# Mixer output and the second feed-forward block: gated sums kept as operands, output weights loaded once, turned rows put in place

## Chip, core and metric

The kernel runs on one core of a Trainium2 chip (trn2). The time is device time in microseconds (us) of one execution of the whole program. The engines are TensorE (PE, matmuls; PEld, its weight loads), VectorE (DVE), ScalarE (ACT), GpSimd (POOL) and SyncE (SP), whose queue issues all of this kernel's DMAs.

## What is computed

One layer of a streaming encoder on 1152 tokens (1024 of a prompt, 8 times 16 of samples), width 1024, all in float32 in and out. Cut to what matters here:

```python
f = swiglu(rms_norm(h, ffn1_pre_g), ffn1_w_gu, ffn1_w_down)   # d_ff 2816
h = h + 0.5 * rms_norm(f, ffn1_post_g)
# mixer: three branches ya, yb, yc out of one input projection
yb = rms_norm(y * silu(z), norm_g)                             # y: the scan
merged = gates[0] * (ya @ wa) + gates[1] * (yb @ wb) + gates[2] * (yc @ wc)
h = h + rms_norm(merged @ wo, mix_post_g)
f = swiglu(rms_norm(h, ffn2_pre_g), ffn2_w_gu, ffn2_w_down)
h = h + 0.5 * rms_norm(f, ffn2_post_g)
```

## The kernel before

Every float32 product is made of three float32r matmuls: both operands are split into a rounded part (`hi`, an ACT copy) and the rest (`lo`, a subtraction on DVE or POOL), `split`, lines 121 to 123. `mm3` issues the three, the one with `lo` weights first.

Tokens come in 9 tiles of 128, in 3 chunks of 384 (`CH`) for projections and down products, and in 2 units of 576 (`UNIT`, each of two halves of 288) for gate/up. `prenorm` normalises a token tile, and its `turn` transposes it on PE into `xT`, split. `gate_up` (line 378) makes gate and up products of one unit in seven half-size products per step (a Strassen-like scheme): per step of 128 columns, `weights` (285) loads two blocks of 0.5 MB into staging buffers and makes seven split combinations on ACT, DVE and POOL, `cell` (324) does the seven products and stores the gated result to DRAM (`hff`). The unit's operands `A0` and `A1` are made once by `operands` (261) from raw transposed rows `xr`: seven splits and four sums of 128x1152, two of these eleven steps and one further subtraction on POOL.

`down` (410) multiplies by a 1024-wide weight: for each chunk of 384 tokens it walks over blocks of k, loads 128 rows of the left operand (`hr`, split into `hh`) and of the weight (`wdraw`, split into `wd`), and runs 18 matmuls of 128x512 for each. `post` then norms each token tile, adds the residual, and `after` may begin the next norm; its transposes run two steps later (`later`, `passed`).

After the scan, `finish` (1020) loads the scan's output `yz`, norms and turns it into `ybT`, fills PE with what is left of the gate products (`filler`, 14 of 24 gates), and runs the branch projection: for each 128 columns j and chunk c, 24 matmuls, a product with the gate, a sum, and a store to DRAM (`mrg`). Then `down` reads `mrg` back, with the output weights `wo` loaded and split anew for each chunk, `lo` on POOL. The new rows are normed, transposed to `xs`, stored to DRAM (`xr`) and loaded again unit by unit for the second `gate_up`, whose first weights are made when the second chunk is done (`between`).

A planner in the framework puts each engine's instructions in order by its own estimates, in the order of the program where they are ready together; buffers of a pool go round, and a new pool's buffer waits for whoever last used that place. Pools stand on the left or right end of the memory, as named.

## Time and profile before

| | us |
|---|---|
| median of 3 runs | 2979.92 |
| lowest and highest run | 2973.94, 2980.82 |
| the profiled execution | 2983.82 |
| its span, first to last instruction | 2982.1 |

The profile's page gives busy time by engine: PE 2825.8 us (95% of the span), its weight loads 2644.9, DVE 1384.5, ACT 1007.5, POOL 847.6. The granted clock of PE was 0.975 on average. In the order of the program: first gate/up loop to about 555 us, first down to about 830, mixer to about 1830, branch projection to 2015, output projection to about 2170, second gate/up loop to 2699, second down to the end. A busy PE is not PE at its peak: what a stretch loses is read by setting its matmuls against their pace in an undisturbed stretch.

### The profile page before, as it was taken

How to read it: one execution, taken by the hardware profiler on the slowest of the kernel's cores; microseconds unless marked ns; L12 is line 12 of the kernel's file. 1: busy time of each engine (PE TensorE's matmuls, PEld its weight loads, DVE VectorE, ACT ScalarE, POOL GpSimd, SP SyncE). 2: the span in 40 equal slices, each digit the busy share in tenths (PEclk: the TensorE clock that was granted, in tenths of full speed). 3: DMA queues.
4: the chain of work that ended last, by engine and by line, in shares of the span. 5: the costliest groups of instructions: out<-in, count | busy, mean ns of one | idle time of the engine just before them, and what ended most of it. 6: DMA issues, size and time to landing. Idle time of an engine off the chain costs nothing. (4 is left out here: it accounts for less than half of the span.)

```text
span 2982.1 us, 43879 instructions
## 1 busy us (share of the span) xinstructions
PE 2825.8 (95%) x17310; PEld 2644.9 (89%) x17310; DVE 1384.5 (46%) x2039; ACT 1007.5 (34%) x1738; POOL 847.6 (28%) x909
## 2 busy tenths in 40 slices
PE   5999999999999999999999997998779999999999
PEld 4999999888899999999988886996569999997887
DVE  6444444454532243222477775422474444445553
ACT  6222222444443113211243455313442222324442
POOL 4443343100010001111066654144443434430000
PEclk8999999999999999999999998999889999999999
DMA  3222221665743114333233356665452222226662
GB/s 117 67 82 71 70 76 55 202 200 184 218 142 104 48 33 118 104 91 94 69 96 105 91 151 184 193 210 179 156 164 71 67 85 71 67 92 203 218 220 93
DMA packets 354268, 362.44 MB, mean 122 GB/s; under 512 B 24447, under 2 KB 306291, under 8 KB 354062
## 3 DMA queue, kind: packets, MB, share of 16 engines
q1 hardware_dynamic: 354061, 359.64, 39.2%
q8 instruction: 136, 2.23, 0.3%
q14 instruction: 71, 0.57, 0.1%
HBM read 280.88 MB, written 78.69 MB: 121 GB/s over the span
## 5 line engine op out<-in xcount | busy, mean ns | idle before, releaser
L204 PE MATMUL down<-wd,hh 128*128 128x512 f32 x2808 | 657.4, 395 | 40.1 <-ACT wd L122 22.2
L204 PEld LDWEIGHTS down<-wd,hh 128*128 128x128 f32 x2808 | 532.7, 191 | 158.7 <-ACT wd L122 26.4
L320 PE MATMUL pw<-A_s,w 128*128 128x288 f32 x4224 | 612.9, 301 | 29.7 <-ACT A_s L122 15.2
L320 PEld LDWEIGHTS pw<-A_s,w 128*128 128x128 f32 x4224 | 580.1, 192 | 40.1 <-ACT A_s L122 16.8
L320 PE MATMUL pw<-A,w 128*128 128x288 f32 x3168 | 457.1, 297 | 13.0 <-DVE A L123 7.7
L320 PEld LDWEIGHTS pw<-A,w 128*128 128x128 f32 x3168 | 435.7, 190 | 15.6 <-DVE A L123 8.8
L204 PE MATMUL pgate<-xT,w_hi 128*128 128x384 f32 x1152 | 295.6, 337 | 0.0
L123 DVE TENSOR_TENSOR w<-wraw,w 128x512 fp32r<-128x512 f32 x220 | 189.5, 863 | 135.2 <-ACT w L122 135.2
L123 DVE TENSOR_TENSOR wd<-wdraw,wd 128x1024 fp32r<-128x1024 f32 x132 | 161.4, 1224 | 118.8 <-ACT wd L122 117.9
L122 ACT CAST wd<-wdraw 128x1024 fp32r<-128x1024 f32 x156 | 163.3, 1050 | 153.4 <-PE down L204 94.0
L204 PEld LDWEIGHTS pgate<-xT,w_hi 128*128 128x128 f32 x1152 | 208.2, 188 | 0.6
L204 PE MATMUL pxbc<-xT,w_hi 128*128 128x384 f32 x768 | 205.5, 345 | 0.0
L204 PE MATMUL pgate<-xT,w_lo 128*128 128x384 f32 x576 | 196.9, 342 | 3.8 <-DVE w_lo L123 3.8
L123 DVE TENSOR_TENSOR w_lo<-wraw,w_hi 128x1024 fp32r<-128x1024 f32 (+1 forms) x104 | 125.5, 1206 | 123.2 <-ACT w_hi L122 110.8
L371 POOL TENSOR_TENSOR wh<-wh,wy 128x288 f32<-128x288 f32 x88 | 89.7, 1019 | 276.1 <-ACT wh L360 247.9
L122 ACT CAST w<-wraw 128x512 fp32r<-128x512 f32 x220 | 135.9, 619 | 78.0 <-PE pw L320 45.1
L161 POOL TENSOR_SCALAR post_r<-post_ss 128x1 f32<-128x1 f32 x27 | 8.1, 300 | 535.8 <-ACT junk L172 535.8
L123 DVE TENSOR_TENSOR hh<-hr,hh 128x384 fp32r<-128x384 f32 x156 | 92.4, 597 | 131.3 <-ACT hh L122 131.3
L122 ACT CAST hh<-hr 128x384 fp32r<-128x384 f32 x156 | 79.2, 512 | 214.1 <-PE down L204 164.3
L204 PEld LDWEIGHTS pxbc<-xT,w_hi 128*128 128x128 f32 x768 | 139.6, 190 | 0.9
L204 PE MATMUL pxbc<-xT,w_lo 128*128 128x384 f32 x384 | 135.8, 354 | 0.0
L345 ACT ACTIVATE wh<-pw 128x288 f32<-128x288 f32 x88 | 36.2, 411 | 280.6 <-PE pw L320 280.6
(270 smaller groups left out, 4175.0 us busy)
## 6 DMA issues: line engine op xcount, KB each, us to landing
wdraw<-in_ffn_w_down_dram SPq DMA_DIRECT2D x132, 512.0 KB
wraw<-in_ffn_w_gu_dram SPq DMA_DIRECT2D x88, 512.0 KB
wraw<-in_w_in_dram SPq DMA_DIRECT2D x80, 512.0 KB
hff<-wh SPq DMA_DIRECT2D x88, 288.0 KB
hr<-hff SPq DMA_DIRECT2D x132, 192.0 KB
wdraw<-in_w_out_dram SPq DMA_DIRECT2D x24, 512.0 KB
h<-fg SPq DMA_DIRECT2D x18, 512.0 KB
cumb<-cumd SPq DMA_DIRECT2D x36, 256.0 KB
```

Of the source, the lines that this page charges most:

```text
L122: self.nc.scalar.copy(hi, raw)
L123: return (eng or self.nc.vector).tensor_tensor(lo, raw, hi.bitcast(F32), op=ALU.subtract)
L161: nc.gpsimd.tensor_scalar(r, ss[0], ss[1], eps, op0=ALU.add, op1=ALU.add)
L204: mm = self.nc.tensor.matmul(ps, lhsT=lhs[a], rhs=rhs[b], start=first and i == 0, stop=last and i == 2)
L320: self.nc.tensor.matmul(ps[:, :HCH], lhsT=b[:, x, k], rhs=a[:, y, k], start=first and k == 0 and i == 0, stop=k == 3 and i == 2, skip_grou ...
L345: nc.scalar.activation(h[:, 0], b[2][:, :HCH], AF.Silu)
L371: nc.gpsimd.tensor_tensor(h[:, 1], h[:, 1], y, op=ALU.mult)
```

## The change

- `finish` no longer stores the gated sums. Each is split into an SBUF tile `mT` (24 tiles of 128x2x384), and `down` takes these as its left operand. The order of the last two column blocks is by chunk. Gates left over are issued ahead of each group of transposes instead of around them.
- The output weights are loaded and split once into 8 tiles `wd` (`lo` on DVE), in the place of `ybT` on the right side, ahead of `down`.
- In the tail, the normed copy goes to the buffer of the residual (`xn`) instead of over the result. Of the transposed rows, those of tokens 0 to 575 go through DRAM as before, into buffers of their own; those of tokens 576 to 1151 are written from PSUM straight to the raw rows of unit 1.
- The first weights of the second gate/up loop are made after the operands of unit 0, in the place of `wd`, instead of during the output projection.
- The last step of the second gate/up loop runs unit 0 before unit 1. `down_pools` places `hh` ahead of `wd`.
- After the mixer there are 3 staging buffers (before: 5) and 5 `aux` buffers (before: 6).

The diff, without hunks that only hand on new arguments:

```diff
...
@@ -224,11 +225,11 @@
-    def prenorm_raw(self, t, h, gcol, put):
+    def prenorm_raw(self, t, h, xn, gcol, put):
         nc = self.nc
         r = self.rsqrt(self.sumsq(h, "pre_ss"), D * EPS, "pre_r")
-        nc.scalar.activation(h, h, AF.Copy, scale=r)
+        nc.scalar.activation(xn, h, AF.Copy, scale=r)
...
@@ -248,8 +249,8 @@
-        def put(t, half):
-            c0 = t * P
+        def put(t, half, skip=0):
+            c0 = t * P + skip
             while c0 < t * P + P:
@@ -375,13 +376,13 @@
-    def gate_up(self, B, a0, second, w_gu, h_d):
+    def gate_up(self, B, a0, second, w_gu, h_d, end):
         A = [a0, None]
         for kt in range(NFF):
             if kt > 0:
                 B = self.weights(w_gu, kt * P, DFF + kt * P)
-            for u in (1, 0) if kt == NFF - 1 else (0, 1):
+            for u in end if kt == NFF - 1 else (0, 1):
                 if A[u] is None:
@@ -390,11 +391,20 @@
-    def down_pools(self, ctx, nwd, nhh=8):
+    def down_pools(self, ctx, nwd):
         self.hrp = self.pool(ctx, "hr", 3)
+        self.hhp = self.pool(ctx, "hh", 8)
         self.wdp = self.pool(ctx, "wd", nwd)
-        self.hhp = self.pool(ctx, "hh", nhh)
-        self.late, self.step = [], 0
+    def from_dram(self, h_d):
+        def hT(k, r):
+            hr = self.hrp.tile([P, CH], F32, name="hr")
+            self.nc.sync.dma_start(hr, h_d[k * P : (k + 1) * P, r * CH : (r + 1) * CH])
+            hh = self.hhp.tile([P, 2, CH], F32R, name="hh")
+            self.split(hr, hh[:, 0], hh[:, 1])
+            return hh
+        return hT
@@ -407,9 +417,15 @@
-    def down(self, h_d, w, post, blocks=DOWN_BLOCKS, wide_eng=None, between=None):
-        nc = self.nc
+    def wide(self, w, k):
+        raw = self.stage("wdraw")
+        self.nc.sync.dma_start(raw, w[k * P : (k + 1) * P, :])
+        wd = self.wdp.tile([P, 2, D], F32R, name="wd")
+        self.split(raw, wd[:, 0], wd[:, 1])
+        return wd
+    def down(self, hT, w, post, blocks=DOWN_BLOCKS):
         end = sum(blocks) - 1
@@ -419,14 +435,8 @@
                 for k in kts:
-                    hr = self.hrp.tile([P, CH], F32, name="hr")
-                    nc.sync.dma_start(hr, h_d[k * P : (k + 1) * P, r * CH : (r + 1) * CH])
-                    hh[k] = self.hhp.tile([P, 2, CH], F32R, name="hh")
-                    self.split(hr, hh[k][:, 0], hh[k][:, 1])
-                    raw = self.stage("wdraw")
-                    nc.sync.dma_start(raw, w[k * P : (k + 1) * P, :])
-                    wd[k] = self.wdp.tile([P, 2, D], F32R, name="wd")
-                    self.split(raw, wd[k][:, 0], wd[k][:, 1], wide_eng)
+                    hh[k] = hT(k, r)
+                    wd[k] = w(k)
                 last = k0 == end + 1
@@ -444,9 +454,6 @@
                     self.passed()
-            if between is not None:
-                between(r)
     def post_norm(self, banks, g, h, fg):
@@ -1017,21 +1024,34 @@
-    def finish(self, m_d):
+    def finish(self, mp):
         n, nc, io = self.n, self.nc, self.io
         ybT = n.new_xT()
-        g_y = n.gain(io["ssm_norm_g"][0], "gpre")
-        for t in range(NT):
-            if t % 3 == 0:
-                self.filler((t // 3 + 1) * KD - self.filled)
-            y = n.aux("yz")
-            nc.sync.dma_start(y, self.yz_d[t * P : (t + 1) * P, :])
-            n.prenorm(t, y, g_y, ybT, y)()
-        ws = {}
+        g_y = n.gain(io["ssm_norm_g"][0], "gpost")
+        def norms(c):
+            out = []
+            for t in range(3 * c, 3 * c + 3):
+                y = n.aux("yz")
+                nc.sync.dma_start(y, self.yz_d[t * P : (t + 1) * P, :])
+                out.append(n.prenorm(t, y, g_y, ybT, y))
+            return out
+        for c in range(2):
+            turns = norms(c)
+            self.filler((4, 5)[c] * KD // 2 - self.filled)
+            for turn in turns:
+                turn()
+        turns = norms(2)
+        self.filler(3 * KD - self.filled)
         order = [(j, c) for j in range(KD) for c in range(NCHK)]
-        order.sort(key=lambda jc: (jc[0] > 1, jc[0] < 2 and jc[1] == 2, jc))
+        order.sort(key=lambda jc: (jc[0] > 1, jc[0] < 2 and jc[1] == 2, jc[0] > 5, jc[1] if jc[0] > 5 else 0, jc))
+        ws, mT = {}, {}
         for j, c in order:
+            if c == 2:
+                while turns:
+                    turns.pop(0)()
             if j not in ws:
@@ -1043,7 +1063,9 @@
             nc.gpsimd.tensor_tensor(s, s, a, op=ALU.add)
-            nc.sync.dma_start(m_d[js, cs], s)
+            m = mT[j, c] = mp[c].tile([P, 2, CH], F32R, name="mT")
+            n.split(s, m[:, 0], m[:, 1])
+        return mT
@@ -1068,13 +1090,12 @@
                 nc.sync.dma_start(dst(t), fg)
-                return after(t, fg)
+                return after(t, fg, h)
         return post
     h_d = dram("hff", [DFF, TOK])
     xr_d = dram("xr", [D, TOK])
-    m_d = dram("mrg", [D, TOK])
     A = [None, None]
...
@@ -1122,9 +1143,9 @@
             n.down(
-                h_d,
-                io["ffn1_w_down"][0],
-                tail(io["ffn1_post_g"][0], 0.5, lambda t: rows(io, t), at(h1), lambda t, h: n.prenorm(t, h, gn, xT, h)),
+                n.from_dram(h_d),
+                lambda k: n.wide(io["ffn1_w_down"][0], k),
+                tail(io["ffn1_post_g"][0], 0.5, lambda t: rows(io, t), at(h1), lambda t, h, xn: n.prenorm(t, h, gn, xT, xn)),
             )
@@ -1151,52 +1172,65 @@
         n.banks(c0, 6)
-        n.stages(c0, 5, 6, 512)
-        cr = ExitStack()
+        n.stages(c0, 3, 5, 512)
+        n.gbp = n.pool(c0, "gb", 1)
+        cx = ExitStack()
+        xrp = n.pool(cx, "xr", 1)
+        XR = [None, {(t, k): xrp.tile(n.blk, F32, name=f"xr{t}{k}") for t in range(2) for k in range(2)}]
+        with ExitStack() as cr:
+            with ExitStack() as cl:
+                mp = [n.pool(cl, f"mT{c}", KD) for c in range(NCHK)]
+                with ExitStack() as cw:
+                    n.conv_pools(cw, "right", 4)
+                    mT = m.finish(mp)
+                ctx_x.close()
+                n.wdp = n.pool(cr, "wd", KD, "right")
+                wo = [n.wide(io["w_out"][0], k) for k in range(KD)]
+                xr0 = n.pool(cr, "xr0", 1, "right")
+                def after(t, h, xn):
+                    n0 = min(max(UNIT - t * P, 0), P)
+                    xs = n.stage("xs").rearrange("p (k c) -> p k c", k=KD) if n0 else None
+                    def put(t, half):
+                        if n0:
+                            yield xs[:, 4 * half : 4 * half + 4, :n0], 0, n0
+                        if n0 < P:
+                            for dst, a, b in n.put_units(XR)(t, half, n0):
+                                yield dst, a, b
+                    turn = n.prenorm_raw(t, h, xn, n.cols["g2"], put)
+                    def out():
+                        turn()
+                        if n0:
+                            nc.sync.dma_start(xr_d[:, t * P : t * P + n0].rearrange("(k p) c -> p k c", p=P), xs[:, :, :n0])
+                    return out
+                n.down(lambda k, r: mT[k, r], lambda k: wo[k], tail(io["mix_post_g"][0], 1.0, at(h1), at(h2), after), (4, 4))
+                n.passed(2)
+            c1 = c0.enter_context(ExitStack())
+            n.unit_pool(c1, 0)
+            XR[0] = {(t, k): xr0.tile(n.blk, F32, name=f"xq{t}{k}") for t in range(2) for k in range(2)}
+            for (t, k), v in XR[0].items():
+                nc.sync.dma_start(v, xr_d[512 * k : 512 * k + 512, t * HCH : (t + 1) * HCH].rearrange("(k p) c -> p k c", p=P))
+            A0 = n.operands(0, XR[0])
+        n.unit_pool(c1, 1)
+        n.turn_pools(c1)
+        with ExitStack() as cr:
+            n.w_pools(cr, "right")
+            B = n.weights(w_gu, 0, DFF)
+            n.gate_up(B, A0, lambda: n.operands(1, XR[1]), w_gu, h_d, (0, 1))
+        c1.close()
+        cx.close()
         with ExitStack() as c1:
-            n.gbp = n.pool(c1, "gb", 1)
-            n.down_pools(c1, 6, 6)
-            with ExitStack() as cw:
-                n.conv_pools(cw, "right", 4)
-                m.finish(m_d)
-            ctx_x.close()
-            n.unit_pool(cr, 0, "right")
-            n.w_pools(cr, "right")
-            made = {}
-            def unit(u):
-                x = n.raw_unit(u)
-                for (t, k), v in x.items():
-                    c = (2 * u + t) * HCH
-                    nc.sync.dma_start(v, xr_d[512 * k : 512 * k + 512, c : c + HCH].rearrange("(k p) c -> p k c", p=P))
-                return n.operands(u, x)
-            def after(t, h):
-                xs = n.stage("xs").rearrange("p (k c) -> p k c", k=KD)
-                turn = n.prenorm_raw(t, h, n.cols["g2"], lambda t, half: [(xs[:, 4 * half : 4 * half + 4], 0, P)])
-                def out():
-                    turn()
-                    nc.sync.dma_start(xr_d[:, t * P : (t + 1) * P].rearrange("(k p) c -> p k c", p=P), xs)
-                return out
-            def between(r):
-                if r == 1:
-                    made["B"] = n.weights(w_gu, 0, DFF)
-            n.down(m_d, io["w_out"][0], tail(io["mix_post_g"][0], 1.0, at(h1), at(h2), after), (4, 4), nc.gpsimd, between)
-            A0 = unit(0)
-            n.passed(2)
-        with ExitStack() as c1:
-            n.unit_pool(c1, 1)
-            n.turn_pools(c1)
-            n.gate_up(made["B"], A0, lambda: unit(1), w_gu, h_d)
-        cr.close()
-        with ExitStack() as c1:
-            n.gbp = n.pool(c1, "gb", 1)
             n.down_pools(c1, 8)
-            n.down(h_d, io["ffn2_w_down"][0], tail(io["ffn2_post_g"][0], 0.5, at(h2), lambda t: out_rows(io, t)))
+            n.down(
+                n.from_dram(h_d),
+                lambda k: n.wide(io["ffn2_w_down"][0], k),
+                tail(io["ffn2_post_g"][0], 0.5, at(h2), lambda t: out_rows(io, t)),
+            )
```

## Rows read from the trace of the kernel before

**Rows 1.** Stretches: length, busy us by engine, granted PE clock, DMA share, GB/s.
```profile
600.00:700.00 100.00, 99.74 (x451) 82.20 (x450) 55.41 (x69) 45.11 (x78) 6.95 (x12) 1.00 0.61 202
...
2100.00:2200.00 100.00, 63.97 (x271) 51.27 (x270) 52.52 (x53) 43.43 (x70) 46.11 (x34) 0.79 0.64 203
...
2800.00:2900.00 100.00, 100.00 (x443) 82.81 (x442) 53.31 (x65) 39.19 (x61) 2.58 (x6) 1.00 0.70 227
```

**Rows 2.** Waits of PE, 2015 to 2225 us: us in total, times, longest.
```profile
PE down L204 <- ACT wd L122: 22.2, 2, 14.2
PE down L204 <- POOL wd L123: 10.6, 8, 2.7
PE pw L320 <- DVE A_s L123: 9.1, 3, 3.6
PE pw L320 <- ACT A_s L122: 4.6, 2, 3.8
```

**Rows 3.** Stretches as in rows 1: branch projection, and the start of the second block.
```profile
1920.00:2015.00 95.00, 95.00 (x550) 95.00 (x549) 28.20 (x36) 15.09 (x18) 40.69 (x29) 1.00 0.65 199
...
2168.00:2218.00 50.00, 29.23 (x146) 26.06 (x144) 43.39 (x32) 22.51 (x29) 25.18 (x13) 0.77 0.63 191
```

**Rows 4.** Chain of work (start, length, what); stretches for tile pw; timeline of PE.
```profile
2015.23 29.29 PE down L204 x129
...
2300.00:2600.00 300.00, 300.00 (x2240) 297.86 (x2239) 60.36 (x134) 21.81 (x54) 1.00 0.24 73
...
2697.23 1.86 PE L320 MATMUL pw<-A_s,w 128*128 128x288 f32 x12 [1.04 <-DVE wy L337]
```

**Rows 5.** Timeline, 1830 to 1850 us: start, length, engine, line, operation; idle before, releaser.
```profile
1842.95 1.94 PE L195 MATMUL tp<-ident,yz 128*128 128x128 f32 x8 [12.67 <-DVE yz L186]
...
1847.79 1.22 DVE L123 TENSOR_TENSOR w_lo<-wraw,w_hi 128x1024 fp32r<-128x1024 f32 x1
```

**Rows 6.** Stretches at the two joints from gate/up to down; timeline of ACT at the second.
```profile
555.00:566.00 11.00, 7.35 (x19) 5.05 (x20) 8.41 (x11) 5.07 (x8) 1.04 (x1) 0.73 0.72 219
2699.00:2710.00 11.00, 7.55 (x19) 4.98 (x19) 9.56 (x13) 6.91 (x10) 1.05 (x1) 0.71 0.68 211
...
2702.96 1.99 ACT L122 CAST wd<-wdraw 128x1024 fp32r<-128x1024 f32 x2 [3.62 <-DMA hff<-wh]
```

**Rows 7.** Groups by line and shape, 1790 to 2260 us: busy us, mean ns; idle before.
```profile
L123 POOL TENSOR_TENSOR wd<-wdraw,wd 128x1024 fp32r<-128x1024 f32 x24 | 58.1, 2437 | 38.4 <-ACT wd L122 38.4
...
L123 DVE TENSOR_TENSOR hh<-hr,hh 128x384 fp32r<-128x384 f32 x24 | 18.6, 780 | 54.4 <-ACT hh L122 54.4
...
L122 ACT CAST hh<-hr 128x384 fp32r<-128x384 f32 x24 | 12.2, 510 | 89.6 <-PE down L204 55.6 <-DMA hr<-mrg 33.9
```

**Rows 8.** Timeline, tail of token tile 0 in the output projection.
```profile
2036.39 0.60 ACT L172 ACTIVATE junk<-down 128x512 bf16<-128x512 f32 x1 [4.24 <-PE down L204]
...
2044.51 1.09 PE L239 MATMUL tp<-ident,fg 128*128 128x128 f32 x8
...
2045.71 1.28 DVE L241 TENSOR_TENSOR xs<-tp,colsg 128x512 f32<-128x512 f32 x2
```

**Rows 9.** Timeline of PE and DVE at the start of the first block.
```profile
27.12 3.25 PE L320 MATMUL pw<-A,w 128*128 128x288 f32 x12 [4.70 <-DVE A L123]
...
57.21 0.68 DVE L241 TENSOR_TENSOR xr<-tp,colsg 128x512 f32<-128x512 f32 x1
...
80.47 6.55 PE L320 MATMUL pw<-A_s,w 128*128 128x288 f32 x48
```

**Rows 10.** Timeline of DVE and POOL at the start of the second block.
```profile
2183.54 3.61 POOL L271 TENSOR_TENSOR xr<-xr,xr 128x1152 f32<-128x1152 f32 x1 [9.90 <-DVE xr L271]
2184.63 3.73 DVE L123 TENSOR_TENSOR A_s<-xr,A_s 128x1152 fp32r<-128x1152 f32 x1
```

**Rows 11.** Timeline, weights of one late gate/up step of the second block.
```profile
2652.77 1.29 POOL L303 TENSOR_TENSOR wt<-wraw 128x512 f32<-128x512 f32 x1
...
2667.43 0.62 ACT L122 CAST w<-wt 128x512 fp32r<-128x512 f32 x1 [0.67 <-PE pw L320]
```

9 lines of the change are left out of this document (5 added, 4 removed).

## The prediction

> **What bounds the kernel now.** I read the table by stretches first. TensorE (PE) is busy all the time at full clock in the long product loops, and around 2100 us it is not: 64 of 100 us busy at clock 0.79, against 100 of 100 at 1.00 in the last block [rows 1]. This is the output projection after the mixer and the start of the second feed-forward block. The waits of PE in 2015 to 2225 us say on what: the four longest entries hold 46.5 us, 32.8 of them on the two halves of the split of `wd` (output weights), and 13.7 on operands `A_s` of the next block [rows 2]. In 2168 to 2218 VectorE (DVE) is busy 43.4 of 50 us and PE's clock stands at 0.77: operands are what ends last there [rows 3].
>
> How much is lost I take from work, not from busy time, since slow clock hides in busy time. From the first `down` matmul (2015.23) to the end of the last product of the gate/up loop (2697.23 + 1.86 = 2699.09) are 683.9 us [rows 4]. In it lie 432 `down` matmuls (8 k x 9 token tiles x 2 x 3), which in the last stage go at 100 us / 443 = 0.2257 us each [rows 1]: 97.5 us; 72 transposes of 1.09 / 8 = 0.136 us [rows 8]: 9.8 us; and 3696 `pw` matmuls (22 steps x 2 units x 7 products x 12) at 300 / 2240 = 0.1339 us [rows 4]: 495.0 us. Together 602.3, so **81.6 us are lost**, in waits and in matmuls run between them at the lower of the two clock levels (1.2 GHz, a granted clock of 0.5).
>
> Three smaller holes: 12.67 us before the first transpose after the scan, and the gate matmuls only from 1849 on, when `w_lo` is ready (1847.79 + 1.22) [rows 5]; and the two joints from gate/up to down, where 19 matmuls take 11 us: 11 - 19 x 0.2257 = 6.7 us lost at each; behind the second, the second `wd` split waits for the last store of the gated sums [rows 6].
>
> **The change part by part.**
> *Weights once, sums kept.* 16 of 24 loads of `wd`, 16 ACT casts of 1.0 us [rows 6] and 16 POOL subtractions (2.44 us) go, 8 subtractions go to DVE, 1.22 us for the same 128x1024 shape [rows 5]; 24 stores and 24 loads of the merged sums go; their 24 splits move from `down` to the branch projection [rows 7]. There they cost ACT 24 x 0.51 = 12 us and DVE 24 x 0.78 = 19 us over 95 us in which DVE was busy 28 [rows 3]: hidden; if that cover were gone, only the last tile's split (1.3 us) could reach PE, and it is first used a third of the way from the end. The 16 wd rounds are what PE waited for: the 32.8 us go with them.
> *What is late next there:* `wd` now lies where the transposed `ybT` lay. By the pool sizes and the way slots are handed out, `wd` 1 to 4 lie over the first two thirds of `ybT`, which the new order (units 6 and 7 chunk by chunk) frees four and two products before the end of the branch loop; but `wd` 0 touches the last third, free only when the last branch matmul is done. So `down` starts a cast and a subtraction late: 1.0 + 1.22 and some 0.2 of signals, 2.5 us. Bounds 0 (another slot) and 15 (its raw load late as well: the longest single wait on `wd` now was 14.2 [rows 2]). The other seven are needed at 1.4 us steps at the earliest, and their splits take 1.22.
> *`down` itself* then has per 128 tokens 48 x 0.2257 + 8 x 0.136 = 11.9 us of PE against about 4 us each of ACT and DVE. I allow 2 us of waits (0 to 8).
> *Units.* Unit 0 (tokens 0 to 575) still goes through DRAM, but its buffers no longer queue behind the tails of the last tokens; its source is complete after token tile 4, with some 25 us of `down` left, so four of seven operands can be made under it; the last two wait for the memory of kept sums that the last matmuls read, and are needed 5th and 7th. The weights of the first gate/up step move from the middle of `down` (where their loads, casts and subtractions take turns with those of `wd` on SP, ACT and POOL) to its last 16 us, over `wd` 1 to 4. Unit 1 now goes from PSUM straight to its place: two stores and two loads of DRAM per half and the queueing on SP disappear. What then ends last is the tail of token tile 8: last matmul, squares, norm, norm, transpose, copy. For tile 0 it took 2036.39 to 2046.99 = 10.6 us [rows 8]. Then unit 1's operands have to be made while PE runs unit 0's first cell (84 x 0.134 = 11.3 us). The trace has the same situation: at the start of the first block the last transposed piece of unit 1 was in place at 57.9 us (57.21 + 0.68), and 167 matmuls of the first two cells lie between the first `pw` row and 80.47, from where PE runs on; 80.47 - 168 x 0.1339 = 58.0. So the loop ran as if it had begun, unhindered, at the moment unit 1 was complete [rows 9]. I take this for the changed kernel: loop begins 10.5 us after the last `down` matmul, of which 24 transposes (3.3 us) are work already counted: 7.2 us lost, bounds 2 and 25.
> Loss of this stage: 2.5 + 2 + 7.2 = 11.7 in place of 81.6: **gain 69.9 us**.
> *A rule set against it.* A subtraction of 128x1152 on DVE, 1.37 us by its size against the 1.22 of 128x1024 [rows 5], took 3.73 while POOL ran one of 3.61 [rows 10]. The Trainium skill, page "SBUF — State Buffer", section "SBUF: two separate sides", says that DVE instructions with two SBUF inputs and GpSimd instructions take a shared port pair as an exclusive lock. The trace agrees: 3.73 is near the sum of waiting and own time. What it does to the transition is the first rival.
> *Gates ahead of turns.* Six, four, four gates go ahead of the three groups of transposes. `w_lo` no longer stands behind DVE's copies of turned rows: about 1.2 us earlier, and the gain of the post norm is loaded later, 0.5 MB less ahead of the `yz` loads; 16 transposes that stood in the hole come later. I take **1 us**, between -4 (three staging buffers instead of five, where the gates load 0.5 MB each) and 6.
> *Joints.* Behind the second block `hr`, `hh` and the first `wd` now lie over unit 1's raw rows and unit 0's operands, free early or 11 us before the end, since unit 0 now goes first at the end; nothing waits for the last store: 6.7 becomes 1.7, **gain 5** (-1 to 6.7). In the first block only the order of `hh` and `wd` changes; the second and third `wd` then wait for gate/up weights of the last products instead of the store: **gain 1.5** (-4 to 6).
> *Nothing:* the norm written beside its input, which takes a wait on a store out of a chain off the path; aux 5 for 6; the final `down` with three staging buffers in place of five: the first `down` has three, and PE is 99.7 us of 100 busy there [rows 1].
>
> Sum: 69.9 + 1 + 5 + 1.5 = 77.4. The profiled execution took 2983.8 (span 2982.1 and 1.7 around it), so 2906.4; the median of the runs is 3.9 below the profiled one: **2902 us**.
>
> **The rivals.**
> 1. *Operands stay the bound.* After the last `down` matmul DVE has, by size from 1.22 and 0.68 [rows 5, 9], six instructions of 128x512 for tile 8 (4.1 us), three of 128x1152 left of unit 0 (4.1), nine for unit 1 (12.3), seven splits of the next weights (4.8) and eight sums of 128x288 (3.1): 28 us; if POOL's two long instructions of 3.6 and four of 1.3 all hold it up, 41. PE has 25.9 us of work there. Loss 15 and some at reduced clock, 22 in place of 7: 2917. For it speaks the DVE of this place now [rows 3, 10]; against it, that the first block has the same work with the same POOL instructions [rows 9].
> 2. *`down` starts late*: raw loads of `wd` behind the loads of branch weights in three buffers, 15 instead of 2.5: 2915. Against: the last branch weight is split six products before the end of that loop.
> 3. *All waits vanish*: 4 lost in place of 11.7, joints at 1, the hole 6: 2883.
> 4. *Slower: three staging buffers starve the second gate/up loop.* A step uses two; the second raw block of the next step can be loaded only when the fourth product's weights are split, some 13 us before its first split is due (now POOL takes it at 2652.77, and the ACT split that needs it comes at 2667.43 [rows 11]). A load that lands within 13 us costs nothing; if it took 18, each of 22 steps would lose 5: 110 less the 77 gained, 3013. It beats the gain from 3.5 us a step on. Against: DMA is 0.24 busy in this loop [rows 4].
> 5. *The change is undone by the planner*, which orders each engine's instructions by its own estimates and already places gates between transposes: that takes only the 1 us of the hole.
>
> **How the numbers follow.** Forecast 2890 to 2912: 0.55; rival 1: 0.17; 2: 0.10; 3: 0.12; 4: 0.04; anything else within 0.3%, or near it: 0.02. The likeliest case gives 2902. The range takes in rivals 1 to 3 and the bounds of the transition: 2880 to 2932. About 0.3% (9 us) is what a measurement of this kernel can tell from no change; faster by more than that 0.94, within it 0.02, slower by more 0.04.
>
> **What would show it.** Right: no wait on `wd` above 3 us; `down` in some 108 us, against some 150 now; PE at clock 1.00 until the last `down` matmul; 8 `wd` rows on DVE at 1.2 us. The first `down` matmul waits on `wd` for about 2.5 us. DVE saturated for some 25 us after `down`, with PE waiting on `A` for 5 to 8 us there. Joint at the second block short. Wrong: waits on `w` in each gate/up step (4), a `wd` load in the chain (2), 15 us or more of waits on `A` (1).

## The result and the profile after

| | before | after |
|---|---|---|
| median of the runs, us | 2978.23 | 2931.99 |
| lowest and highest run | 2973.94, 2980.82 | 2931.33, 2933.2 |
| profiled execution, its span | 2983.82, 2982.1 | 2931.51, 2929.8 |

The ratio is 0.9851, interval 0.9835 to 0.9868: faster by 46 us, where 77 were forecast. 2931.99 lies 30 us above the forecast and at the very end of its range; from the 2979.92 that the forecast started at, the ratio gives 2935.5, just outside. Cut at the same places in both traces, the profiled executions say where the gain is and where it is not:

| part, us | before | after | gained | forecast |
|---|---|---|---|---|
| start to the mixer's first matmul | 875.8 | 880.6 | -4.8 | 1.5 |
| from there to the first projection `down` | 1139.2 | 1126.9 | 12.4 | 1 |
| projection, first to last `down` matmul | 150.8 | 113.1 | 37.7 | |
| last of these to the end of the gate/up loop | 533.2 | 532.9 | 0.3 | |
| the two lines above together | 684.0 | 646.0 | 38.0 | 69.9 |
| end of that loop to the last matmul | 276.7 | 271.6 | 5.0 | 5 |

(The very first loop comes to full clock up to 3.7 us sooner or later from one execution to the next, whatever the edit. In the first line this is taken out by the `pw` matmuls done by 500 us: 3298 before, 3314 after, 16 x 0.1339 = 2.1 us added to 878.5.)

The stretches of the kernel after, with the columns of [rows 1]:

```profile
600.00:700.00 100.00, 98.25 (x445) 80.94 (x444) 54.52 (x69) 44.33 (x76) 6.66 (x12) 1.00 0.60 198
...
2005.00:2119.00 114.00, 109.87 (x492) 86.71 (x493) 41.02 (x59) 39.52 (x83) 16.24 (x35) 1.00 0.49 156
2119.00:2167.00 48.00, 22.83 (x129) 21.58 (x128) 40.98 (x37) 27.32 (x39) 27.55 (x14) 0.72 0.15 47
2167.00:2651.00 484.00, 481.33 (x3585) 477.95 (x3584) 210.39 (x371) 141.11 (x283) 176.49 (x169) 0.99 0.25 77
```

And most of the projection in the kernel before:

```profile
2015.00:2160.00 145.00, 109.79 (x462) 86.02 (x461) 50.43 (x67) 58.14 (x109) 64.45 (x52) 0.87 0.49 166
```

The projection is what was hoped: PE busy 110 of 114 us at clock 1.00, where it was 110 of 145 at 0.87. Behind it stands a hole as wide as the old one [rows 3]: PE busy 23 of 48 us at 0.72, DVE 41. The waits of PE from 2004 to 2225 us (total, times, longest) name what ends last there:

```profile
PE tp L240 <- ACT h L232: 13.1, 9, 9.3
PE pw L321 <- DVE w L124: 12.9, 2, 11.2
PE pw L321 <- DVE wy L338: 2.5, 1, 2.5
PE down L205 <- ACT wd L123: 1.1, 1, 1.1
```

The waits on `wd` and on `A_s` of [rows 2] are gone but for 1.1 us. In their place come the tail of the last token tile (`h`) and the first step's weights `w`. PE's timeline shows where: one `down` matmul wait at the beginning, then the two long ones, 11 and 27 us behind the last `down` matmul (2112.54 + 5.86 = 2118.40):

```profile
2005.34 28.84 PE L205 MATMUL down<-wd,mT 128*128 128x512 f32 x120 [1.13 <-ACT wd L123]
...
2112.54 5.86 PE L205 MATMUL down<-wd,mT 128*128 128x512 f32 x24
...
2129.03 1.97 PE L240 MATMUL tp<-ident,h 128*128 128x128 f32 x8 [9.32 <-ACT h L232]
...
2144.94 3.22 PE L321 MATMUL pw<-A,w 128*128 128x288 f32 x12 [11.22 <-DVE w L124]
```

Why DVE comes to `w` so late is seen on ACT and SP. `xq` is unit 0's raw rows, from which its operands are made:

```profile
2054.26 1.90 SPq L1217 DMA_DIRECT2D xq<-xr  x2
...
2088.41 0.91 SPq L1217 DMA_DIRECT2D xq<-xr  x2
```

```profile
2104.60 0.60 ACT L173 ACTIVATE junk<-down 128x512 bf16<-128x512 f32 x1 [17.41 <-PE down L205]
...
2119.75 3.25 ACT L123 CAST A<-xq 128x1152 fp32r<-128x1152 f32 x3
```

The loads are issued at 2054 and 2088, yet the first operand cast runs at 2119.75, and ACT stands idle for 17.4 us ahead of 2104.60. The three casts wait for nothing but the loads. They stand behind the squares of token tile 8 in ACT's instruction order, as the built program lists it (DMAHW: waits for a load; PE: for a matmul):

```
L173 ACTIVATE junk_19217,post_ss_19216<-down_19029 128x512 [waits PE_49]
L173 ACTIVATE junk_19221,post_ss_19220<-down_19033 128x512 [waits PE_49,Activation_49]
L123 CAST A0_11_19278<-xq00_19270 128x1152 [waits DMAHW5_49]
```

In the layout of after, the operands `A0` lie in a new pool over the memory of the sums `mT`, which the last `down` matmuls read. My theory: the planner takes the new pool's place to be free only with the whole old pool, so that it ordered all of unit 0's operands behind the last matmuls, although each buffer was free earlier. The rivals: POOL instructions that hold up DVE (rival 1 of the prediction), the order of the first weights, and the place of those weights over `wd`. Two more places ask for a cause: the gain of 12 us ahead of the projection, and the loss of 5 in the first block.

### The profile page after: what moved, and what is told of

The parts are those of the page before. It is cut to its first block, busy times and chain, and to the rows that moved or that the text cites. A ratio compares the mean times of both kernels' runs of the same rounds, so it can differ in the third digit from the quotient of the medians.

```text
span 2929.8 us, 43686 instructions
## 1 busy us (share of the span) xinstructions
PE 2810.5 (96%) x17310; PEld 2633.5 (90%) x17310; DVE 1377.3 (47%) x2051; ACT 992.5 (34%) x1722; POOL 770.2 (26%) x885
## 5 line engine op out<-in xcount | busy, mean ns | idle before, releaser
L321 PE MATMUL pw<-A_s,w 128*128 128x288 f32 x4224 | 606.7, 300 | 20.7 <-ACT A_s L123 10.6
L205 PE MATMUL down<-wd,hh 128*128 128x512 f32 x2376 | 545.0, 391 | 5.1 <-ACT wd L123 4.7
L205 PEld LDWEIGHTS down<-wd,hh 128*128 128x128 f32 x2376 | 447.1, 189 | 99.9 <-ACT wd L123 5.5
L321 PE MATMUL pw<-A,w 128*128 128x288 f32 x3168 | 456.5, 298 | 19.7 <-DVE w L124 12.9
L124 DVE TENSOR_TENSOR w<-wraw,w 128x512 fp32r<-128x512 f32 x220 | 180.3, 821 | 134.9 <-ACT w L123 134.8
L124 DVE TENSOR_TENSOR wd<-wdraw,wd 128x1024 fp32r<-128x1024 f32 x140 | 172.0, 1232 | 133.7 <-ACT wd L123 133.4
L123 ACT CAST wd<-wdraw 128x1024 fp32r<-128x1024 f32 x140 | 146.6, 1051 | 143.7 <-PE down L205 92.1
L124 DVE TENSOR_TENSOR w_lo<-wraw,w_hi 128x1024 fp32r<-128x1024 f32 (+1 forms) x104 | 125.8, 1210 | 118.9 <-ACT w_hi L123 106.3
L372 POOL TENSOR_TENSOR wh<-wh,wy 128x288 f32<-128x288 f32 x88 | 81.3, 923 | 210.5 <-ACT wh L361 184.4
L123 ACT CAST w_hi<-wraw 128x1024 fp32r<-128x1024 f32 (+1 forms) x104 | 102.2, 983 | 83.9 <-PE pyw L205 45.9
L338 DVE TENSOR_TENSOR wx<-wx,pw 128x288 f32<-128x288 f32 x176 | 79.5, 452 | 100.7 <-PE pw L321 100.2
```

What stands on the lines that cost most here:

```text
L123: self.nc.scalar.copy(hi, raw)
L124: return (eng or self.nc.vector).tensor_tensor(lo, raw, hi.bitcast(F32), op=ALU.subtract)
L205: mm = self.nc.tensor.matmul(ps, lhsT=lhs[a], rhs=rhs[b], start=first and i == 0, stop=last and i == 2)
L321: self.nc.tensor.matmul(ps[:, :HCH], lhsT=b[:, x, k], rhs=a[:, y, k], start=first and k == 0 and i == 0, stop=k == 3 and i == 2, skip_grou ...
L338: nc.vector.tensor_tensor(o, i, b[k][:, :HCH], op=ALU.add)
L372: nc.gpsimd.tensor_tensor(h[:, 1], h[:, 1], y, op=ALU.mult)
```

## The experiments

Each ran against the kernel before on the same chip; times are medians, the ratio is to the kernel before, and stretches are cut as in the table above; "the stage" is the projection and the second gate/up loop together, from the first projection `down` to the end of that loop. A stretch is read from one profiled execution. Kernels with the same code for it show the scatter: 879.5 to 882.0 us up to the mixer's first matmul (nine kernels with after's code there), 1121.8 to 1128.8 from there to `down` (six), 646.0 to 648.7 in the stage (four). An edit starts from the kernel after unless it says otherwise.

### The hole behind the scan

*gates_only*: the kernel before with only the new order of gates and turned rows in `finish`.

```diff
+        for c in range(2):
+            turns = norms(c)
+            self.filler((4, 5)[c] * KD // 2 - self.filled)
+            for turn in turns:
+                turn()
```

> The kernel before with one part of the change: gates ahead of the turns of the gated norm. The prediction gave this part 1 us (-4 to 6): it took the ready time of the gates' weights (w_lo at 1847.8) as given. In the kernel after, the stretch from a common matmul of the scan (1808.09 before, 1809.00 after) to the first down matmul went from 207.1 to 196.3 us, 10.8 less. Theory: the gates' order alone does that, because their weights are now loaded ahead of the stores at the end of the scan: 8 to 12 us faster than before, no wait of 12.7 us on yz, clock 1.00 there. Rival (the gain needs the smaller pools or the sums kept in SBUF): 0 to 3 us.

Measured 2982.56, 1.0015 (1.0004 to 1.0026): no gain, rather a loss of 4 us. From the mixer's first matmul to `down` it took 1143.3 us against 1139.2, and a wait of 12.1 us on `yz` was still there.

*three_stages*: the kernel before with three staging buffers (and five `aux`); *gates_three_stages*: both edits.

```diff
-        n.stages(c0, 5, 6, 512)
+        n.stages(c0, 3, 5, 512)
```

> The kernel before with three staging and five aux buffers in place of five and six in its second half, as the change has them, and nothing else of the change. In before the five staging buffers reach over the memory of the aux tiles that the end of the scan still stores from; with three they lie exactly where the scan's own staging buffers lay. Theory (the planner hands memory over by whole pools, so the gates' weights can be loaded before 1830 only if their staging pool overlaps nothing of the scan's end, and the gates must also stand ahead of the turns): alone no gain in the hole, as the first eight gates are the only ones ahead of the first turns; 0 to 3 us. Rival (the buffers alone do it): 8 to 12 us faster than before. Fewer buffers could also cost in the output projection: 0 to 5 us.

> The kernel before with the gates ahead of the turns (which alone changed nothing: 12.1 us of wait on yz stayed, with the weights loaded from 1829 on) and with three staging and five aux buffers. Theory (order and memory are both needed): the gates' weights are loaded from about 1806 on, the wait of 12 us on yz goes, the stretch from the scan to the first down matmul falls from 207 to some 197 us: 8 to 12 us faster than before. Rival (the gain in the kernel after comes from something else, such as fewer stores): 0 to 3 us.

Measured 2966.19, 0.9963 (0.9948 to 0.9977), and 2969.57, 0.9970 (0.9960 to 0.9980). The stretch took 1121.3 and 1128.3 us: fewer buffers, without the gates, bring 17.9 us of it, more than even the rival expected, and the new order of gates costs 7.0 of these again. SP issues the weights of the gates (`wraw`) at these times, first before, then three_stages:

```profile
1834.99 14.46 SPq L130 DMA_DIRECT2D wraw<-in_w_in_dram  x6
```

```profile
1801.22 1.06 SPq L130 DMA_DIRECT2D wraw<-in_w_in_dram  x2
1809.74 1.07 SPq L130 DMA_DIRECT2D wraw<-in_w_in_dram  x2
```

and the first transpose of `yz` behind the scan waits 1.37 us instead of 12.67 [rows 5]:

```profile
1841.92 1.06 PE L195 MATMUL tp<-ident,yz 128*128 128x128 f32 x8 [1.37 <-DVE yz L186]
```

In the built program of before, five staging buffers reach over bytes 3648 to 24128 of a partition, and the scan's last stores read from tiles at 15936 to 24128; three buffers end at 15936. So I read it that late tiles under two of the five held back the loads; the SP rows show that the loads moved, but no run moved those tiles alone. The gate/up loop was not starved: the stage took 685.2 us, against 684.0 before.

*gates_back*: after with the old order of gates and turned rows.

> The kernel after with the gates and the turns of the gated norm in the order of the kernel before; all else as after. On before, the smaller buffers alone shortened the stretch from the first pz matmul to the first down matmul by some 17 us, with the gates ahead as well by 9, and the gates alone made it 4 longer. Theory (the gain in this stretch is the memory of the staging buffers; the gates ahead cost 4 to 8 us of it, as a wait of 3.5 us on w_lo and slow clock behind it show): 4 to 8 us faster than the kernel after. Rival (with the sums kept in SBUF the order is needed): 0 to 10 us slower.

Measured 2929.45, 0.9833 (0.9814 to 0.9852); the stretch took 1122.8 against 1126.9. In after the gates that now go first wait for `w_lo` (1840 to 2010 us):

```profile
PE pgate L205 <- DVE w_lo L124: 4.6, 3, 3.5
```

That wait is gone in gates_back. Its 4.1 us are within the scatter (norm_back, with after's order, took 1121.8), but the later kernels agree: the three on shared buffers with after's order took 1127.6 to 1128.9, the five with the old order (and the first block's edits undone) 1119.5 to 1124.9. So the order of gates costs some 5 us, and the buffers alone make the gain.

### The start of the second block

*no_gpsimd*: POOL's steps of the second block's operands and of its first weights on DVE. *w21_second*: the first step's seven weights made in the order 11, 21, t1, t2, t4, t3, 22, so that the second product's weights come second.

```diff
+            A0 = n.operands(0, XR[0], nc.vector)
+            B = n.weights(w_gu, 0, DFF, nc.vector)
+            n.gate_up(B, A0, lambda: n.operands(1, XR[1], nc.vector), w_gu, h_d, (0, 1))
```

> The kernel after, with the GpSimd instructions of the second block's operands (two of 128x1152 per unit) and of its first weights (four of 128x512) given to VectorE. Theory (the two engines hold each other up on a shared port): 16 us of GpSimd time that blocks VectorE (2 x (2.65 + 2.83) + 4 x 1.29) become 8.2 us of VectorE (4 x 1.35 + 4 x 0.69), the norm of the last token tile isn't held up (2.86 us instead of 0.86 for its two GpSimd instructions), and the kernel is 5 to 9 us faster than the kernel after. Rival (they run side by side, and GpSimd relieves VectorE): 3 to 8 us slower.

> The kernel after, with the weights of the first gate/up step of the second block made in the order in which the first cell uses them: 21 second instead of fifth, t4 ahead of t3. Theory (the order of the weights sets when PE runs on: 11.2 us of wait on w ahead of the second product): the second product runs about 10 us earlier, the wait on w falls below 4 us, and the kernel is 4 to 8 us faster than the kernel after. Rival (VectorE and GpSimd have more to do after the last down matmul than PE can cover, whatever the order): the wait moves to t4 or to operands, 0 to 2 us.

Measured 2930.95, 0.9842 (0.9824 to 0.9860), and 2927.61, 0.9835 (0.9817 to 0.9852). Behind the last `down` matmul they took 530.9 and 531.9 us against 532.9 (three more kernels with after's code there: 534.2 to 535.5). In w21_second the wait of 11.22 us falls apart into two, and PE waits 8.6 us for `w` in all instead of 12.9. But it waits more for the tail and for `wx`, so that all its waits from 2004 us on sum to 28.8 instead of 30.0:

```profile
2140.22 2.92 PE L333 MATMUL pw<-A,w 128*128 128x288 f32 x12 [2.59 <-DVE w L124]
...
2149.15 3.25 PE L333 MATMUL pw<-A,w 128*128 128x288 f32 x12 [6.00 <-DVE w L124]
```

In no_gpsimd DVE has more to do, and the wait grows to 13.82 us:

```profile
2150.34 3.25 PE L321 MATMUL pw<-A,w 128*128 128x288 f32 x12 [13.82 <-DVE w L124]
```

So taking POOL out brings 2 to 5 us here and the order of weights 1 to 4, both short of what was expected of them: neither sets the bulk of the 35 us lost.

*shared_slots*: sums and operands of unit 0 take turns in one pool of eight equal buffers, so that each is handed over by itself (the eighth later holds the loop's working tiles).

```diff
+        n.ap[0] = n.pool(cx, "mA", KD)
...
-                mp = [n.pool(cl, f"mT{c}", KD) for c in range(NCHK)]
+                mp = [n.ap[0].tile([P, 3, 2, CH], F32R, name="mT", tag="mA") for _ in range(KD)]
+                n.a0tag = "mA"
...
-            n.unit_pool(c1, 0)
...
+        n.evb = n.ap[0].tile([P, 2, 4, HCH], F32, name="ev", tag="mA")
```

> The kernel after, with the kept sums and unit 0's operands in one pool of eight slots of 9216 bytes (three sums or one operand each), so that an operand can follow the sums of its slot alone; the working tiles of the cells take the eighth slot. Theory (the planner places unit 0's operands behind the last down matmul because their pool follows the sums' pools as a whole, though the first five wait for nothing there): seven of nine VectorE instructions of unit 0 (9.5 us) and its two GpSimd ones (5.5 us, which hold VectorE up) move under down, VectorE is busy some 30 us in place of 41 in the 48 us behind it, and the kernel is 9 to 12 us faster than the kernel after. Rival (the tail of the last token tile, unit 1 and the first weights alone set the start): 0 to 3 us.

*shared_w21*: the same with the weights' order of w21_second.

> As shared_slots, and the first weights in the order in which the first cell uses them (alone that gave about 1 us of the stage). Theory (with unit 0's operands out of the way the weights of the second and third product are what PE waits for): 3 to 6 us faster than shared_slots. Rival (VectorE's total still ends last, with unit 1's operands): 0 to 2 us.

Measured 2928.02, 0.9833 (0.9818 to 0.9847), and 2926.40, 0.9827 (0.9812 to 0.9841). The stage fell from 646.0 to 634.1 and 633.0, the stretch behind `down` from 532.9 to 516.3 and 515.2. ACT in shared_slots now makes the first operands as soon as their loads have landed, the first 61 us earlier, and all seven are split before the last `down` matmul ends at 2123.35; in after none is:

```profile
2058.57 1.16 ACT L124 CAST A<-xq 128x1152 fp32r<-128x1152 f32 x1 [9.48 <-DMA xq<-xr]
...
2094.98 1.16 ACT L124 CAST A<-xq 128x1152 fp32r<-128x1152 f32 x1 [7.59 <-DMA xq<-xr]
```

```profile
2119.00:2167.00 48.00, 34.81 (x208) 31.79 (x206) 36.96 (x42) 26.95 (x44) 25.36 (x18) 0.86 0.24 76
```

In the same 48 us PE does 208 matmuls instead of 129, at 0.86 instead of 0.72. `down` itself is now 4.7 us longer (113.1 to 117.8); near its end one transpose waits 4 us for a normed row, beside the operands' work:

```profile
2115.08 1.43 PE L241 MATMUL tp<-ident,h 128*128 128x128 f32 x8 [4.06 <-ACT h L233]
```

So 11.9 us of the stage are left, and 6.9 are lost behind the gate/up loop (271.6 to 278.6): the first `wd` buffer there lies over the loop's working tiles, and its cast waits for the last store out of them.

```profile
2644.55 1.04 ACT L124 CAST wd<-wdraw 128x1024 fp32r<-128x1024 f32 x1 [6.42 <-DMA hff<-ev]
```

*shared_joint*: shared_slots with the last `down` pools in the old order, `wd` ahead of `hh`.

```diff
         self.hrp = self.pool(ctx, "hr", 3)
+        if first:
+            self.wdp = self.pool(ctx, "wd", nwd)
         self.hhp = self.pool(ctx, "hh", 8)
```

> As shared_slots, with the wd buffers of the last down below the hh buffers. In shared_slots the output projection and the second gate/up loop took 634.1 us against 646.0 in the kernel after, 11.9 less, but its last joint waited 6.0 us on wd, whose first buffer lay over the working tiles of the cells until their last store. Theory (the 11.9 us are there, and the joint gave 5 of them back): that wait falls below 2 us and the kernel is 8 to 12 us faster than the kernel after. Rival (the time moves on to another wait): 2 to 5 us, as shared_slots.

Measured 2924.04, 0.9811 (0.9793 to 0.9828): the last part takes 274.1 instead of 278.6, so 4.4 come back. Of the edits to after so far this is the first whose interval lies wholly below after's (0.9835 to 0.9868); the others are told apart by their stretches alone.

### The first block

*norm_back*: the first block's norm over its input again; *pools_back*: the first `down` pools in the old order.

```diff
-                tail(io["ffn1_post_g"][0], 0.5, lambda t: rows(io, t), at(h1), lambda t, h, xn: n.prenorm(t, h, gn, xT, xn)),
+                tail(io["ffn1_post_g"][0], 0.5, lambda t: rows(io, t), at(h1), lambda t, h, xn: n.prenorm(t, h, gn, xT, h)),
```

> The kernel after with one edit undone: the norm behind the first down writes its result over its input again. Up to the first pz matmul the kernels with the change are some 5 us later than those without, set to the same start of the first loop; 2 of them in the joint and in down, where the transposes wait 4.6 us on the norm in place of 1.3, and 2 behind it. Theory (the other buffer makes the norm late): 3 to 5 us faster than the kernel after, the waits on the norm near 1.3 us. Rival (it is the order of hh and wd): 0 to 1 us.

> The kernel after with one edit undone: in the first block wd's buffers lie below hh's again. Theory (that order sets the joint: in after the first down matmul waits 3.9 us on wd, in before 1.1, 1.9 and 0.7 us on hh and wd at three places): the waits are those of before, and the kernel is 0 to 1 us faster than the kernel after, as the whole joint differs by 0.5 us. Rival (the order sets the waits on the norm in down as well): 3 to 5 us faster.

Measured 2928.69, 0.9827 (0.9809 to 0.9844), and 2930.36, 0.9836 (0.9819 to 0.9853). The mixer's first matmul came at 877.9 and 878.6 against 880.6 in after and 875.8 before: 2.8 and 2.0 of the 4.8 us lost. Both lie below the nine kernels with both edits (879.5 to 882.0); the five below with neither came at 875.8 to 877.1. In norm_back PE's waits for the norm between 560 and 885 us fall from 4.6 to 2.3 us; what pools_back changes in the waits is not clear.

### All of it together

*combined*: shared_slots, the weights' order, and the old pools, gates and norm. *combined_w0*: also the first three weights needed in a pool of their own, away from `wd`. *combined_dve*: combined with unit 1's operands and the first weights without POOL. *w0_dve*: combined_w0 and that.

```diff
+                n.w0p = n.pool(cx, "W0", 3, "right")
-            b = self.wp.tile([P, 2, 4, P], F32R, name="w2")
+            b = (self.w0p if self.w0p and name in ("11", "21", "22") else self.wp).tile([P, 2, 4, P], F32R, name="w2")
```

> The kernel after with all that helped alone: shared slots with the joint mended, gates and turns, norm and first pools as in before, first weights in the order of use. Theory (the parts lie at different places and add up; against the kernel after the stage lengths gave 11.6 for the slots, less 2.5 in the joint, 4 for the gates, 3 to 8 for the norm, 2 for the pools, 1 for the weights): 2908 to 2914 us. Rival (the three edits that give the first part back share one gain): 2915 to 2919.

> As combined, with memory of their own, free during down, for the three first weights that are plain splits (11, 21, 22), so that they can be made under down. In shared_slots PE waited 4.3 us on w and worked at the lower clock level for some 15 us behind down, and the stretch from the last down matmul to the end of the loop still lost 516.3 less 497.2, 19 us. Theory (first weights are what is late there): the wait on w goes, the stretch is 5 to 8 us shorter than in combined, and so is the time. Rival (the tail of the last token tile and unit 1's operands are late, whatever the weights do): 0 to 2 us.

> As combined, with GpSimd's part of unit 1's operands and of the first weights on VectorE. Theory (with fewer VectorE instructions left behind down, what GpSimd holds up there matters as it did alone, 2 us, or more): 1 to 4 us faster than combined. Rival (VectorE is now short of time for unit 1): 0 to 3 us slower.

> combined_w0 and combined_dve together: three first weights made under down, and GpSimd's part of unit 1's operands and of the first weights on VectorE. Alone they shortened the output projection and the loop behind it from 635.1 to 630.6 and 631.4 us. Theory (two causes at two places: weights late at the first product, and two engines holding each other up at unit 1): they add, 626 to 628 us and 2900 to 2905 in all. Rival (both relieve VectorE of the same wait): 630 us, 2906 as combined_w0.

| | us | ratio | stage | `down` | behind it |
|---|---|---|---|---|---|
| combined | 2913.32 | 0.9771 (0.9756 to 0.9785) | 635.1 | 118.9 | 516.2 |
| combined_w0 | 2906.20 | 0.9748 (0.9734 to 0.9763) | 630.6 | 118.2 | 512.5 |
| combined_dve | 2911.33 | 0.9756 (0.9740 to 0.9773) | 631.4 | 119.0 | 512.5 |
| w0_dve | 2907.53 | 0.9760 (0.9744 to 0.9776) | 628.9 | 118.5 | 510.4 |

PE behind `down` in combined_w0: the transposes of the last tile wait 3.9 us instead of 9.3, and twelve matmuls of unit 0 run ahead of them.

```profile
2114.31 1.84 PE L336 MATMUL pw<-A,w 128*128 128x288 f32 x12
...
2123.26 1.97 PE L242 MATMUL tp<-ident,h 128*128 128x128 f32 x8 [3.87 <-ACT h L234]
...
2126.67 3.25 PE L336 MATMUL pw<-A,w 128*128 128x288 f32 x12 [1.45 <-DVE w L126]
```

combined_w0 beats both kernels: 75 us under the one before by its ratio, where 77 were forecast of the change. The two last edits bring 4.5 and 3.7 us of the stage each on its own, and 6.2 together. Some 2 us of this can be scatter: shared_slots, shared_w21, shared_joint and combined took 633.0 to 635.1. By their medians, combined and combined_dve can't be told apart, nor can combined_w0 and w0_dve.

### The pace of the projection's matmuls

After's projection runs slower than before's with nothing waiting: 96 matmuls in a row at 22.74 / 96 = 0.2369 us, against 29.29 / 129 = 0.2271 [rows 4].

```profile
2049.77 22.74 PE L205 MATMUL down<-wd,mT 128*128 128x512 f32 x96
```

Three kernels move `wd`. *aligned*: 32 bytes lower. *wd_left*: to the left side, next to the sums. *w0_dve_place*: w0_dve with the pool `xr0` and 32 bytes ahead of `wd`, which puts `wd` at nearly the place of wd_left.

```diff
+                n.pool(cr, "pad", 1, "right").tile([P, 8], F32, name="pad")
```

```diff
-                n.wdp = n.pool(cr, "wd", KD, "right")
+                n.wdp = n.pool(cl, "wd", KD)
```

> The kernel after with 32 bytes of padding under the output weights, so that they start at multiples of 64 bytes as those of both feed-forward blocks do; in the kernel after they start 32 bytes off. There a matmul of the output projection takes 22.74 us / 96 = 0.2369 against 76.89 / 338 = 0.2275 in the first block. Theory (the start address of the moving operand costs it): 0.2275 each, 432 x 0.0094 = 4.1 us faster than the kernel after. Rival (it is something else of this stage, such as operands that stay resident): 0.237 as before, no gain.

> The kernel after with the output weights at another place of SBUF (132672 to 198208 in place of 163808 to 229344, at multiples of 64 bytes), to see the pace of the output projection alone: 0.2369 us a matmul in after, 0.2348 with 64-byte alignment at the old place, 0.2275 in the first block, whose weights lie below 160000. Theory (the place in SBUF costs it): 0.2275 to 0.231. Rival (it is the operands that stay resident, or the order of reads): 0.235.

> As w0_dve, with the output weights at the place in SBUF that let the projection's matmuls run at 22.03 us per 96 in place of 22.74 (133056 up, below unit 0's rows), 64-byte aligned. Theory (432 matmuls gain 3.2 us, but the first weight tile now lies over tiles of the last branch products: its cast comes about 3 us later, as the wait of 4.0 in place of 1.1 us there showed): down itself 3 us shorter, the wait ahead of it 3 longer, the same as w0_dve within 2 us. Rival (the start can be hidden): 3 us faster than w0_dve.

Measured 2934.39, 0.9850 (0.9833 to 0.9867) for aligned; 2945.20 in one execution for wd_left; 2917.44, 0.9791 (0.9776 to 0.9805) for w0_dve_place. The same 96 matmuls in the three, in this order:

```profile
2052.08 22.54 PE L205 MATMUL down<-wd,mT 128*128 128x512 f32 x96
```

```profile
2054.58 22.03 PE L205 MATMUL down<-wd,mT 128*128 128x512 f32 x96
```

```profile
2045.01 22.56 PE L207 MATMUL down<-wd,mT 128*128 128x512 f32 x96
```

| | first byte of `wd` | that, modulo 512 | us each |
|---|---|---|---|
| after | 163808 | 480 | 0.2369 |
| aligned | 163776 | 448 | 0.2348 |
| w0_dve_place | 133056 | 448 | 0.2350 |
| wd_left | 132672 | 64 | 0.2295 |

That low memory is faster fell with w0_dve_place; that 64-byte alignment is all of it fell with aligned, which brings a fifth. What goes along with the pace is the start within 512 bytes, and before's `wd` started at 64 as well. w0_dve fits in: its `wd` starts at 151520, 480 modulo 512, and the median step from one matmul to the next is 0.234 us, as in after; it is 0.232 in the two kernels at 448 and 0.227 at 64. No run changed the start alone at one place, so the cause stays open. wd_left is slower as a whole: its first gate/up weights come later still (a wait on `w` of 21.12 us); w0_dve_place lost 6.4 us of the stage to w0_dve, for a cause that no run isolates.

## Why the prediction was right and wrong

- **The projection: right.** Waits on `wd` were 1.13 us (2.5 forecast; 15 in rival 2, which falls), `wd` is split eight times on DVE at 1280 ns, the sums' splits (24 at 514 ns on ACT and 555 on DVE, less than the 780 I took) are hidden, and the clock stays at 1.00 to the last matmul. `down` took 113.1 us where 432 x 0.2257 + 56 x 0.136 = 105.1 are work: 8.0 lost, 2 forecast. The term that was mis-sized is the pace: 0.2257 was taken from another stage; at 0.2369, 4.8 of the 8 are in the matmuls themselves. Seven waits of transposes on `h` make 3.5.
- **The transition: wrong, and nearly all of the miss.** The forecast let the loop begin, as if unhindered, 10.5 us after the last `down` matmul. It ended 532.9 us after it; less 495.0 of work, that is a start, in effect, at 37.9. (Of the transposes 16 run behind that matmul, not the 24 that I took; the loss by my reckoning is 35.7 in place of 7.2.) The tail of token tile 8 is 13.3 of the 37.9, as its last copy shows; the other 24.6 come after unit 1 was complete, where the first block [rows 9] had none.

```profile
2131.04 0.69 DVE L242 TENSOR_TENSOR xr<-tp,colsg 128x512 f32<-128x512 f32 x1 [0.16 <-PE tp L240]
```

  The step that failed is "four of seven operands can be made under it": none was. The data was there, as I said (in shared_slots the same loads, issued within 0.3 us of after's, had landed by 2058.6 and 2095.0), but I asked when data and memory come free, not where the instructions stand in ACT's order. shared_slots changes the handing over (and with it the place of the loop's working tiles), moves the first cast from 2119.75 to 2058.57, makes all seven under `down` and takes 16.6 us off this stretch. That the order held the casts back is shown by ACT's rows and by what the casts wait for. That the planner chose this order because it hands memory over pool by pool fits shared_slots, and is my theory.
- **"The weights of the first gate/up step move ... to its last 16 us, over `wd` 1 to 4": wrong likewise.** They are made behind the operands, and PE waits for them for 12.9 us. A place of their own brings 3.7 us more behind `down` (combined to combined_w0, 516.2 to 512.5). Even there the loop begins 17.5 us after the last `down` matmul, 7.0 later than forecast: with the operands out of the way the analogy with the first block was still too good. What these 7.0 are was not isolated.
- **Rival 1** had the right place and queue (DVE 41 of 48 us busy) and 22 us in place of 7; but it left three DVE instructions of unit 0 for this place, where all nine ran, and POOL's share was the lesser one. It is there to see:

```profile
2122.89 3.89 DVE L124 TENSOR_TENSOR A<-xq,A 128x1152 fp32r<-128x1152 f32 x3
```

```profile
2124.85 2.01 POOL L162 TENSOR_SCALAR pre_r<-pre_ss 128x1 f32<-128x1 f32 x1 [3.94 <-ACT junk L173]
```

  A POOL instruction on 128x1 took 2.01 us there, the same form 0.31 on average over the kernel (27 `post_r`, 313 ns), in the chain from squares to `h` that PE waits for. The Trainium skill, page "SBUF — State Buffer", section "SBUF: two separate sides", states that a DVE instruction with two SBUF inputs and a GpSimd instruction that reads SBUF shut each other out of a shared port pair for the whole instruction. The trace agrees that it was held up, 2.01 against 0.31, though by more than the 1.3 us of one of DVE's three splits. But no_gpsimd, which empties POOL of all long instructions here, gains only 2 to 5 us behind `down`.
- **Rivals 3, 4 and 5 fall.** Waits are left (3, whose terms add up to 2885 and not 2883); from 2200 to 2600 us 750 or 751 `pw` matmuls run in each 100 us at clock 1.00, and 748 in three_stages from 2300 on, as before (4). The gates stayed where the edit put them (5); the planner did undo a part of the change, but at another place, with unit 0's operands.
- **Gates ahead of turns, +1 forecast, 12.4 measured: right sign, wrong cause.** I took the time at which `w_lo` is ready as given and asked only what stands in front of it on DVE. SP's rows say that its raw load is late; why lies, as I read the layout, in the memory under the staging buffers. My lower bound of -4 "with three staging buffers" was just the part that gains 17.9. The order itself costs 4 to 7 (gates_only, gates_three_stages, gates_back). That the sign came out was luck, and these 11 us more than forecast hide as much of the transition's miss in the total.
- **First joint, +1.5 forecast; the first part lost 4.8.** Two edits share it: the pools' order, which I had put at a gain, and `xn`, which I had put under "Nothing". norm_back brings 2.8 and pools_back 2.0 of it, by one profiled execution each.
- **Second joint: right**, 5.0 of 5. The first `down` follows the last `pw` matmul without a gap:

```profile
2648.41 2.93 PE L321 MATMUL pw<-A_s,w 128*128 128x288 f32 x12 [2.67 <-DVE wy L338]
2651.14 3.29 PE L205 MATMUL down<-wd,hh 128*128 128x512 f32 x11
```

The parts add up to 50.6 us, and the medians differ by 46.2: the terms are of single profiled executions, and that of before lay 5.6 us above its median here.

## What to carry to other kernels

When new buffers take old memory, ask what the planner believes: if a place is handed over pool by pool, the first use of the new pool is ordered behind the last use of the old one on every engine, and buffers that take turns in one pool gave 12 us of the stage here (5 of the whole, until the joint that they made late was mended). A load that comes late may be held by a tile that lies under its staging buffer (argued from the layout here); look at where the tiles lie before an order of instructions is changed. And an engine that is idle for 17 us beside work whose data has landed is the sign of an order, not of a lack of speed.

## What the hardware showed

The pace of a matmul with 512 columns went along with where its moving operand starts: 0.2271 to 0.2295 us with a start at 64 modulo 512 bytes, 0.2348 to 0.2369 at 448 and 480, 2 to 4%, on 432 matmuls 2 to 4 us. That the start is the cause is not shown. And a small POOL instruction in a chain is not cheap beside long DVE splits: 2.01 us in after and 3.97 in no_gpsimd, in place of 0.31:

```profile
2125.82 3.97 POOL L162 TENSOR_SCALAR pre_r<-pre_ss 128x1 f32<-128x1 f32 x1 [3.95 <-ACT junk L173]
```
